# Up-projection in seven products: product 6 taken into the next pair, product 5 in a bank of its own, raw weights of odd pairs in other buffers

## The chip, the core and the metric

The kernel runs on one core of a Trainium2 chip. The core has five engines that work side by side and wait for each other by semaphores: TensorE (PE, matrix products into PSUM), VectorE (DVE), ScalarE (ACT), GpSimd (POOL) and SyncE (SP, which here issues the DMA transfers). Each engine takes its instructions in order. SBUF holds the tiles, PSUM has eight banks of 128 x 512 float32. The metric is the device time of one execution in microseconds (us); lower is better.

## What is computed

The reference is one decoder block on 1024 positions of width 1024: two token mixers (a gated linear attention and an indexed sparse attention), a gated MLP with a short convolution, and a gate with per-layer input, each followed by a layer norm. The change touches the up-projection of the MLP alone:

```python
h = causal_dwconv(x @ w_up[i], conv_w[i], conv_b[i])   # w_up: 1024 x 5632, conv over 3 positions
h_gate, h_val = jnp.split(h, 2, axis=-1)               # 2816 columns each
ffn = (jax.nn.silu(h_gate) * h_val) @ w_down[i]
x = layer_norm(DEEPNORM_ALPHA * x + ffn, ln2_g[i], ln2_b[i])
```

Everything is float32.

## The kernel before

**Precision.** A float32 product is made of three matmuls of a narrower float type: each operand is split into hi (ACT copies it into the narrower type, line 101) and lo (what is left, line 106, here on POOL), and `mm3` (L155 is the matmul) adds hi x hi, hi x lo and lo x hi in PSUM.

**Seven products.** The up-projection works on 22 pairs f of 128-column blocks, a gate block and its value block. A pair is a 2 x 2 block product (two column blocks, two halves of the 1024 positions, two halves of the inner dimension), done in Strassen's way (Winograd's form) with seven products in place of eight. Product j takes a weight part W[j] and an x part XS[j]; the XS are made once, at the end of the layer norm before. One product is 4 inner tiles of 3 matmuls, 12 matmuls of 512 columns, so a pair has 84.

**Weights of a pair** (`w_sets`). Two loads of 512 KB from w_up (line 991) go to two raw tiles wr, of which there are two in all. `left_operands` then alternates between splitting a raw quarter or a difference into hi and lo (put) and making the next difference in place on VectorE (line 164). The order of the parts is 0, 5, 1, 2, 3, 4, 6. There are seven sets of hi and lo tiles (wh and wl), so a part can be written when PE is done with the same part of the pair before.

**Products of a pair** (`up`). Three PSUM banks A, B, Dk (tag ch, eight banks in all). A takes product 0, and later 4 on top; B takes 1, then 3 on top, then 5 on top; Dk takes 2, then 6 on top. Between them the banks are read: s1 = copy of A (ACT, L1022), u2 = s1 + B, u3 = s1 + B after product 3, and four results go to the two halves of h (VectorE, `plus`, L1019; ACT, L1032). Since 3 is added to B, it waits for u2; since 5 is added to B, it waits for u3.

**Convolution** (`conv`). For either half of h: ACT makes the first tap with the bias (L1043), VectorE adds two shifted taps (L1045), the gate half goes through SiLU on ACT (L1048), POOL multiplies gate and value (L164, cv), and SP stores the result to d_act in DRAM (L1050). The last pair's convolution is put off into the next stage.

**Next stage.** The down-projection loads the stored activations into raw tiles ar (three of them, `rawp`), weights into dr, and splits both into units au and wu in the same manner; these lie where the x parts and weight parts were.

**What sets the order.** The kernel's text says what depends on what; a scheduler with its own time model then writes a fixed order for each engine, in which it may pull instructions ahead. So the order rows below and not the code alone tell what an engine does next.

Of the kernel before, what the change touches and what calls it, by code (L numbers as in the profile page):

```python
# [8 lines left out]
F32 = mybir.dt.float32  # L9
# [3 lines left out]
AF = mybir.ActivationFunctionType  # L13
ALU = mybir.AluOpType
# [3 lines left out]
P = 128  # L18
L = 1024
D = 1024  # L20
NT = L // P
KT = D // P
HALF = 512
# [5 lines left out]
NF = FF // P  # L29
# [11 lines left out]
def hybrid_block(ctx: ExitStack, tc: tile.TileContext, x, p, w_in, w_gate_up, b_gate, g_gla, w_gla,  # L41
                 g_ckv, w_uv, w_dsa, w_out, ln1_g, ln1_b, w_up, conv_w, conv_b, w_down, ln2_g, ln2_b,
                 w_ple, w_ple_gate, ln3_g, ln3_b, out, tap=None):
    nc = tc.nc
    V, S, G, T = nc.vector, nc.scalar, nc.gpsimd, nc.tensor
    tap = tap or (lambda name, ap: None)
    x, p, out = x[0], p[0, 0], out[0]
# [11 lines left out]
    wp = pool("wstream")  # L59
# [30 lines left out]
    def nm(s):  # L90
        uid[0] += 1
        return f"{s}_{uid[0]}"

    def bank(kind="mm", shape=(P, HALF)):
        return PS[kind].tile(list(shape), F32, name=nm(kind), tag=kind)
# [119 lines left out]
    def quad(a):  # L215
        return a.rearrange("p (a b) -> p a b", b=P)
# [16 lines left out]
    def run(steps):  # L233
        for f in steps:
            f()
# [64 lines left out]
    with ExitStack() as mix:  # L300
# [359 lines left out]
        with ExitStack() as c3:  # L660
# [138 lines left out]
            for h in range(DH):  # L799
                b = 4 * h - 2.0 * h / (DH - 1)  # L800
# [174 lines left out]
    with ExitStack() as c1:  # L975
        psum_banks(c1, "d", ch=8)
        fp = pool("ffwork", stack=c1)
        rawp = pool("raws", stack=segd, side="right")
        wk = pool("upwork", stack=segk, side="right")
        UE, UE0, US = 'GGGGGGG', 'VVGVVGV', 'VVVV'  # L980
        nset = [0]

        def blocks(f):

            return (NF + f, f) if f < NF - 1 else (f, NF + f)

        def w_sets(f):
            raw = []
            for c in blocks(f):
                raw.append(wp.tile([P, 1024], F32, name=nm("wr"), tag="wr", bufs=2))  # L990
                nc.sync.dma_start(raw[-1].rearrange("p (k c) -> p k c", k=KT), wup_v[:, :, c * P:(c + 1) * P])
            W = []
            for _ in range(7):
                n = nset[0] % 7
                nset[0] += 1
                pl, nb = (wq, 4) if n < 4 else (fp, 3)
                W.append([pl.tile([P, 512], F32R, name=nm(x), tag=x, bufs=nb) for x in ("wh", "wl")])
            run(left_operands(raw[1][:, :512], raw[1][:, 512:], raw[0][:, :512], raw[0][:, 512:],
                              lambda j, src: split(*W[j], src, "A", (UE if f else UE0)[j]), US))
            return [[quad(t) for t in w] for w in W]  # L1000

        def up(f):


            W = w_sets(f)
            h = wk.tile([P, 2, L], F32, name=nm("h"), tag="h")
            hv = [h[:, i].rearrange("p (a g q) -> p a g q", g=2, q=P) for i in range(2)]
            A, B, Dk = (bank("ch") for _ in range(3))

            def prod(ps, j, start):  # L1010
                for k in range(4):
                    mm3(ps, (W[j][0][:, k], W[j][1][:, k]), (XS[j][:, 0, k], XS[j][:, 1, k]), start and k == 0, k == 3,
                        not start)

            def tmp():
                return wk.tile([P, HALF], F32, name=nm("um"), tag="um", bufs=4)

            def plus(out, a, b):
                V.tensor_tensor(out=out, in0=quad(a), in1=quad(b), op=ALU.add)  # L1019
            prod(A, 0, True)  # L1020
            s1 = tmp()
            S.activation(s1, A, AF.Copy)  # L1022
            prod(B, 1, True)
            u2 = tmp()
            plus(quad(u2), s1, B)
            prod(Dk, 2, True)
            prod(B, 3, False)
            u3 = tmp()
            plus(quad(u3), s1, B)
            plus(hv[1][:, :, 1], u3, Dk)  # L1030
            prod(A, 4, False)
            S.activation(hv[0][:, :, 0], quad(A), AF.Copy)  # L1032
            prod(B, 5, False)
            plus(hv[1][:, :, 0], s1, B)
            prod(Dk, 6, False)
            plus(hv[0][:, :, 1], u2, Dk)

            def conv():
                out_ = {}
                for i in (1, 0):  # L1040
                    c = blocks(f)[1 - i]
                    o = out_[c // NF] = wk.tile([P, L], F32, name=nm("cv"), tag="cv", bufs=3)
                    S.activation(o, h[:, i], AF.Identity, bias=cbias[:, c:c + 1], scale=cw[:, 2, c:c + 1])  # L1043
                    for d in (1, 2):
                        V.scalar_tensor_tensor(o[:, d:], h[:, i, :L - d], cw[:, 2 - d, c:c + 1], o[:, d:], ALU.mult,  # L1045
                                               ALU.add)
                    if c < NF:
                        S.activation(o, o, AF.Silu)  # L1048
                sums(out_[0], out_[0], out_[1], ALU.mult, "G")
                nc.sync.dma_start(d_act[f // 6][:, f % 6], out_[0])  # L1050
            return conv

        for f in range(NF):
            last_conv = up(f)
            if f < NF - 1:
                last_conv()
    segx.close()
    sega.close()

# [244 lines left out]
```

## Time and profile before

| | us |
|---|---|
| median of 3 runs (lowest, highest) | 2181.69 (2181.13, 2181.78) |
| the profiled execution, its own time | 2181.69 |
| its span, first to last instruction | 2180.0 |
| up-projection, PE's stretch in the trace | 1306 to 1760 |

A timeline row has the start, the time of the merged run of equal instructions, the engine, the line of the kernel, the operation, output <- inputs by the program's names, sizes, the count, and in brackets the idle time of the engine before it with what ended it. PE's matmuls overlap: a row shows 0.39 us for one, but the next starts earlier, so the pace is read from start to start. VectorE's instructions overlap in the same way by less than 0.1 us. A wait is put down to the releaser that came last.

### The profile page before, as it was taken

To read this page: it belongs to the slowest core of one execution; us is meant where nothing else is said; L and a number is where in the kernel's file an instruction comes from. 1 tells how busy PE (TensorE), PEld (TensorE's weight loads), DVE (VectorE), ACT (ScalarE), POOL (GpSimd) and SP (SyncE) were. 2 spreads that over 40 slices of the span, in tenths; PEclk is the share of its full clock that TensorE was granted. 3 is DMA by queue.
4 is the path that set the end of the run, shared out by engine and by line. 5 is a ranking of instruction groups with operands and counts; after the bars stand their busy time and mean duration, and the time that the engine had idled before them with its cause. 6 is when DMAs were issued, how large, how long until landed. Compare 5 with 4: busy or idle time off the path is not lost.

```text
span 2180.0 us, 32423 instructions
## 1 busy us (share of the span) xinstructions
PE 2066.6 (95%) x12210; PEld 1813.0 (83%) x12210; DVE 1581.1 (73%) x2700; ACT 848.4 (39%) x1498; POOL 956.6 (44%) x808
## 2 busy tenths in 40 slices
PE   9999999999999999998999969999999968989897
PEld 8888899999988888887789967777777768989897
DVE  3489999999138888775243685666676689896965
ACT  4343212222127666665222343444334443332421
POOL 2433443543521212122332775555555655444743
PEclk9999999999999999999999979999999989999999
DMA  4222211211227767779666432232222224224222
GB/s 136 78 68 76 82 42 45 61 50 51 73 82 134 148 134 150 134 172 223 191 201 137 146 108 76 71 118 78 69 86 78 68 82 160 88 74 136 88 98 78
DMA packets 377565, 227.13 MB, mean 104 GB/s; under 512 B 189328, under 2 KB 351760, under 8 KB 377408
## 3 DMA queue, kind: packets, MB, share of 16 engines
q1 hardware_dynamic: 377408, 225.06, 38.2%
q8 instruction: 96, 1.57, 0.3%
q14 instruction: 61, 0.50, 0.1%
HBM read 146.37 MB, written 40.89 MB: 86 GB/s over the span
## 4 chain that ended last, share of the span: by engine, by line
PE 18%; DVE 16%; POOL 9%; DMA 6%; issue 4%; ACT 2%; SPq 0%; POOLq 0%; DVEq 0%; ACTq 0%
PE mm L155 12%; POOL wl L106 6%; DVE wr L164 5%; PE ch L155 5%; DMA wr<-in_w_up_dram 3%; DVE au L106 2%; ACT wh L101 2%; DVE wu L106 1%; DVE ar L164 1%; DVE um L164 1%; DMA wr<-d_ob 1%; DVE dr L164 1%; DVE res_all L1132 1%; DVE cv L1045 1%; POOL lnmv L212 1%
## 5 line engine op out<-in xcount | busy, mean ns | idle before, releaser
L106 POOL TENSOR_TENSOR wl<-wr,wh 128x512 fp32r<-128x512 f32 x381 | 524.9, 1393 | 439.9 <-ACT wh L101 425.2
L155 PE MATMUL ch<-xs,wh 128*128 128x512 f32 x1232 | 385.3, 395 | 33.2 <-DVE um L1019 26.2
L155 PE MATMUL mm<-Ah,wh 128*128 128x512 f32 x832 | 331.6, 399 | 2.0 <-ACT wh L101 1.1
L155 PE MATMUL mm<-Al,wh 128*128 128x512 f32 x832 | 330.4, 397 | 0.8 <-DVE Al L106 0.5
L155 PE MATMUL mm<-Ah,wl 128*128 128x512 f32 x832 | 329.3, 396 | 0.0
L155 PEld LDWEIGHTS ch<-xs,wh 128*128 128x128 f32 x1232 | 231.5, 190 | 91.2 <-DVE um L1019 35.1
L101 ACT ACTIVATE wh<-wr 128x512 fp32r<-128x512 f32 (+1 forms) x278 | 166.9, 625 | 347.1 <-DVE wr L164 144.5
L103 POOL TENSOR_SCALAR wh<-wr 128x512 fp32r<-128x512 f32 x112 | 77.0, 690 | 382.2 <-PE mm L155 211.9
L155 PE MATMUL ch<-xs,wl 128*128 128x512 f32 x616 | 240.8, 392 | 0.8 <-POOL wl L106 0.6
L155 PE MATMUL ch<-wu,au 128*128 128x256 f32 x1512 | 195.1, 291 | 32.3 <-DVE um L164 9.9
L155 PE MATMUL mm<-wl,Ah 128*128 128x256 f32 x768 | 217.6, 285 | 4.5 <-POOL wl L106 4.3
L155 PEld LDWEIGHTS ch<-wu,au 128*128 128x128 f32 x1512 | 189.5, 198 | 38.0 <-DVE um L164 12.1
L155 PE MATMUL mm<-wh,Al 128*128 128x256 f32 x768 | 216.3, 284 | 0.0
L155 PE MATMUL mm<-wh,Ah 128*128 128x256 f32 x768 | 213.8, 284 | 0.0
L155 PEld LDWEIGHTS mm<-Ah,wl 128*128 128x128 f32 x832 | 156.2, 188 | 32.9
L155 PEld LDWEIGHTS mm<-Ah,wh 128*128 128x128 f32 x832 | 156.3, 188 | 32.8 <-ACT wh L101 1.6
L155 PEld LDWEIGHTS mm<-Al,wh 128*128 128x128 f32 x832 | 156.4, 188 | 31.3 <-DVE Al L106 0.9
L651 DVE MATCH_REPLACE8 score<-m,score 128x896 f32<-128x896 f32 (+3 forms) x192 | 166.4, 869 | 0.0
L650 DVE MAX8 m<-score 128x8 f32<-128x896 f32 (+3 forms) x192 | 163.5, 875 | 2.3 <-POOL score L457 2.1
L164 DVE TENSOR_TENSOR wr<-wr,wr 128x512 f32<-128x512 f32 x66 | 88.8, 1346 | 93.9 <-POOL wl L106 93.7
L155 PEld LDWEIGHTS mm<-wl,Ah 128*128 128x128 f32 x768 | 145.7, 190 | 6.2 <-POOL wl L106 5.5
L155 PE MATMUL mm<-wh,au 128*128 128x256 f32 x768 | 144.3, 284 | 2.6 <-ACT wh L101 1.4
(259 smaller groups left out, 4221.0 us busy)
## 6 DMA issues: line engine op xcount, KB each, us to landing
wr<-in_w_in_dram SPq DMA_DIRECT2D x60, 512.0 KB, 3.9
wr<-in_w_up_dram SPq DMA_DIRECT2D x44, 512.0 KB, 3.9
d_act<-cv SPq DMA_DIRECT2D x22, 512.0 KB, 2.6
dr<-in_w_down_dram SPq DMA_DIRECT2D x12, 768.0 KB, 6.4
ar<-d_act SPq DMA_DIRECT2D x12, 768.0 KB, 5.2
d_tg<-tg SPq DMA_DIRECT2D x32, 256.0 KB, 2.0
wr<-in_w_out_dram SPq DMA_DIRECT2D x16, 512.0 KB, 3.6
wr<-in_w_ple_gate_dram SPq DMA_DIRECT2D x16, 512.0 KB, 4.2
```

The costliest lines, as they stand in the source:

```text
L101: S.activation(dst, src, AF.Copy, scale=scale)
L103: (V if eng == "V" else G).tensor_scalar(dst, src, scale, 0.0, ALU.mult, ALU.add)
L106: done["GV"[eng != "G"]] = (G if eng == "G" else V).tensor_tensor(out=dst, in0=src, in1=hi.bitcast(F32), op=ALU.subtract)
L155: T.matmul(ps, lhsT=l, rhs=r, start=start, stop=stop, skip_group_check=more)
L164: (G if eng == "G" else V).tensor_tensor(out=out, in0=a, in1=b, op=op)
L212: G.tensor_scalar(dst, src, scale, eps, ALU.mult, ALU.add)
L650: V.max(m8, score[t])
L651: V.match_replace(score[t], m8, score[t], TAKEN)
L1045: V.scalar_tensor_tensor(o[:, d:], h[:, i, :L - d], cw[:, 2 - d, c:c + 1], o[:, d:], ALU.mult, ALU.add)
L1132: V.scalar_tensor_tensor(rv, rv, ALPHA, src, ALU.mult, ALU.add)
```

## The change

Raw weights of odd pairs are loaded into the ar tiles instead of wr. A pair now uses four banks: product 5 has its own (C). The pair's steps are functions that the loop puts in a row: products 0 and 1 of a pair, then product 6 of the pair before, product 5, the convolution of the pair before's block 0, products 2, 3, 4, and the convolution of the pair's block 1, which is complete after product 3. The um tiles go; the results are summed in place in h, which is two tiles per pair with two buffers each.

```diff
@@ -987,7 +987,11 @@
         def w_sets(f):
             raw = []
             for c in blocks(f):
-                raw.append(wp.tile([P, 1024], F32, name=nm("wr"), tag="wr", bufs=2))
+                if f % 2:
+                    raw.append(rawp.tile([P, 6, 256], F32, name=nm("ar"), tag="ar", bufs=3)
+                               .rearrange("p a b -> p (a b)")[:, :1024])
+                else:
+                    raw.append(wp.tile([P, 1024], F32, name=nm("wr"), tag="wr", bufs=2))
                 nc.sync.dma_start(raw[-1].rearrange("p (k c) -> p k c", k=KT), wup_v[:, :, c * P:(c + 1) * P])
             W = []
             for _ in range(7):
@@ -1002,58 +1006,81 @@
         def up(f):
 
 
+
+
             W = w_sets(f)
-            h = wk.tile([P, 2, L], F32, name=nm("h"), tag="h")
-            hv = [h[:, i].rearrange("p (a g q) -> p a g q", g=2, q=P) for i in range(2)]
-            A, B, Dk = (bank("ch") for _ in range(3))
+            st, out_ = {}, {}
 
             def prod(ps, j, start):
                 for k in range(4):
                     mm3(ps, (W[j][0][:, k], W[j][1][:, k]), (XS[j][:, 0, k], XS[j][:, 1, k]), start and k == 0, k == 3,
                         not start)
 
-            def tmp():
-                return wk.tile([P, HALF], F32, name=nm("um"), tag="um", bufs=4)
-
             def plus(out, a, b):
-                V.tensor_tensor(out=out, in0=quad(a), in1=quad(b), op=ALU.add)
-            prod(A, 0, True)
-            s1 = tmp()
-            S.activation(s1, A, AF.Copy)
-            prod(B, 1, True)
-            u2 = tmp()
-            plus(quad(u2), s1, B)
-            prod(Dk, 2, True)
-            prod(B, 3, False)
-            u3 = tmp()
-            plus(quad(u3), s1, B)
-            plus(hv[1][:, :, 1], u3, Dk)
-            prod(A, 4, False)
-            S.activation(hv[0][:, :, 0], quad(A), AF.Copy)
-            prod(B, 5, False)
-            plus(hv[1][:, :, 0], s1, B)
-            prod(Dk, 6, False)
-            plus(hv[0][:, :, 1], u2, Dk)
-
-            def conv():
-                out_ = {}
-                for i in (1, 0):
-                    c = blocks(f)[1 - i]
-                    o = out_[c // NF] = wk.tile([P, L], F32, name=nm("cv"), tag="cv", bufs=3)
-                    S.activation(o, h[:, i], AF.Identity, bias=cbias[:, c:c + 1], scale=cw[:, 2, c:c + 1])
-                    for d in (1, 2):
-                        V.scalar_tensor_tensor(o[:, d:], h[:, i, :L - d], cw[:, 2 - d, c:c + 1], o[:, d:], ALU.mult,
-                                               ALU.add)
-                    if c < NF:
-                        S.activation(o, o, AF.Silu)
+                V.tensor_tensor(out=out, in0=a, in1=quad(b), op=ALU.add)
+
+            def p0():
+                st["A"] = bank("ch")
+                prod(st["A"], 0, True)
+                st["h"] = [wk.tile([P, L], F32, name=nm("h"), tag=f"h{i}", bufs=2) for i in range(2)]
+                st["hv"] = [h.rearrange("p (a g q) -> p g a q", g=2, q=P) for h in st["h"]]
+                S.activation(st["hv"][1][:, 0], quad(st["A"]), AF.Copy)
+
+            def p1():
+                st["B"] = bank("ch")
+                prod(st["B"], 1, True)
+                plus(st["hv"][0][:, 1], st["hv"][1][:, 0], st["B"])
+
+            def p5():
+                st["C"] = bank("ch")
+                prod(st["C"], 5, True)
+
+            def p2():
+                st["D"] = bank("ch")
+                prod(st["D"], 2, True)
+
+            def p3():
+                prod(st["B"], 3, False)
+                s1, u3 = st["hv"][1][:, 0], st["hv"][1][:, 1]
+                plus(u3, s1, st["B"])
+                plus(s1, u3, st["C"])
+                plus(u3, u3, st["D"])
+
+            def p4():
+                prod(st["A"], 4, False)
+                S.activation(st["hv"][0][:, 0], quad(st["A"]), AF.Copy)
+
+            def p6():
+                prod(st["D"], 6, False)
+                o = st["hv"][0][:, 1]
+                plus(o, o, st["D"])
+
+            def conv(i):
+                c = blocks(f)[1 - i]
+                h = st["h"][i]
+                o = out_[c // NF] = wk.tile([P, L], F32, name=nm("cv"), tag="cv", bufs=3)
+                S.activation(o, h, AF.Identity, bias=cbias[:, c:c + 1], scale=cw[:, 2, c:c + 1])
+                for d in (1, 2):
+                    V.scalar_tensor_tensor(o[:, d:], h[:, :L - d], cw[:, 2 - d, c:c + 1], o[:, d:], ALU.mult, ALU.add)
+                if c < NF:
+                    S.activation(o, o, AF.Silu)
+
+            def conv1():
+                conv(1)
+
+            def conv0():
+                conv(0)
                 sums(out_[0], out_[0], out_[1], ALU.mult, "G")
                 nc.sync.dma_start(d_act[f // 6][:, f % 6], out_[0])
-            return conv
-
+            return p0, p1, p5, p2, p3, p4, conv1, p6, conv0
+
+        late = []
         for f in range(NF):
-            last_conv = up(f)
-            if f < NF - 1:
-                last_conv()
+            p0, p1, p5, p2, p3, p4, conv1, *rest = up(f)
+            run([p0, p1, *late[:1], p5, *late[1:], p2, p3, p4, conv1])
+            late = rest
+        late[0]()
+        last_conv = late[1]
     segx.close()
     sega.close()
 
```

On PE, the place is where product 0 of the next pair ends, in the middle of the stage (ch_14675 is bank B of a pair, xs_11727 the x part of product 0, xs_12438 that of product 5). Before:

```order
L155 MATMUL ch_14819<-xs_11727,wl_14787 128x512
L155 MATMUL ch_14819<-xs_11727,wh_14786 128x512 x2
L155 MATMUL ch_14819<-xs_11727,wl_14787 128x512
L155 MATMUL ch_14675<-xs_12438,wh_14651 128x512 x2
L155 MATMUL ch_14675<-xs_12438,wl_14652 128x512
```

After (ch_14802 is bank B of this pair, ch_14829 its bank C, ch_14705 bank D of the pair before; xs_11728 belongs to product 1, xs_12439 to product 6):

```order
L155 MATMUL ch_14786<-xs_11727,wl_14755 128x512
L155 MATMUL ch_14802<-xs_11728,wh_14756 128x512 x2
L155 MATMUL ch_14829<-xs_12438,wh_14764 128x512 x2
L155 MATMUL ch_14829<-xs_12438,wl_14765 128x512
L155 MATMUL ch_14829<-xs_12438,wh_14764 128x512
L155 MATMUL ch_14705<-xs_12439,wh_14622 128x512
L155 MATMUL ch_14802<-xs_11728,wl_14757 128x512
```

Before, product 0 of the next pair stood between products 3 and 5 of a pair; now product 0 is followed by the start of products 1 and 5 of its own pair and product 6 of the pair before, and bank B takes only products 1 and 3.

On VectorE, one pair's round in the middle of the stage (ch_14675 is bank B, ch_14676 bank Dk; wr_14784 and wr_14782 are the raw weights of the pair that follows). Before:

```order
L164 TENSOR_TENSOR wr_14784<-wr_14784,wr_14782 128x512
L164 TENSOR_TENSOR wr_14782<-wr_14782 128x512
L1019 TENSOR_TENSOR um_14729<-um_14689,ch_14675 128x512
L164 TENSOR_TENSOR wr_14782<-wr_14782,wr_14784 128x512
L1019 TENSOR_TENSOR h_14673<-um_14729,ch_14676 128x4x128
L1019 TENSOR_TENSOR h_14673<-um_14689,ch_14675 128x4x128
L164 TENSOR_TENSOR wr_14784<-wr_14784,wr_14782 128x512
L1045 SCALAR_TENSOR_TENSOR cv_14771<-h_14673,cw,cv_14771 128x1023
```

After (wr_14752 and wr_14750 are the raw weights of the pair that follows; h_14511 and cv_14698 belong to the pair before; ch_14658, ch_14685, ch_14705 are banks B, C, D):

```order
L164 TENSOR_TENSOR wr_14752<-wr_14752,wr_14750 128x512
L164 TENSOR_TENSOR wr_14750<-wr_14750 128x512
L1020 TENSOR_TENSOR h_14655<-h_14656,ch_14658 128x4x128
L1020 TENSOR_TENSOR h_14511<-h_14511,ch_14561 128x4x128
L1064 SCALAR_TENSOR_TENSOR cv_14698<-h_14511,cw,cv_14698 128x1023
L1064 SCALAR_TENSOR_TENSOR cv_14698<-h_14511,cw,cv_14698 128x1022
L164 TENSOR_TENSOR wr_14750<-wr_14750,wr_14752 128x512
L1020 TENSOR_TENSOR h_14656<-h_14656,ch_14658 128x4x128
L1020 TENSOR_TENSOR h_14656<-h_14656,ch_14685 128x4x128
L1020 TENSOR_TENSOR h_14656<-h_14656,ch_14705 128x4x128
L1064 SCALAR_TENSOR_TENSOR cv_14746<-h_14656,cw,cv_14746 128x1023
L1064 SCALAR_TENSOR_TENSOR cv_14746<-h_14656,cw,cv_14746 128x1022
```

The two first differences of the next pair's weights stood ahead of u3; now they stand ahead of the add of product 1, and the three adds behind product 3 stand in one piece with the block's taps behind them.

On POOL, the same round after (wl_14623 is lo part 6 of a pair, the other wl are the parts of the pair that follows in the order 0, 5, 1, 2, 3, 4, cv_14698 the product of gate and value of the pair before):

```order
L106 TENSOR_TENSOR wl_14755<-wr_14752,wh_14754 128x512
L106 TENSOR_TENSOR wl_14623<-ar_14608,wh_14622 128x512
L106 TENSOR_TENSOR wl_14765<-wr_14750,wh_14764 128x512
L164 TENSOR_TENSOR cv_14698<-cv_14698,cv_14602 128x1024
L106 TENSOR_TENSOR wl_14757<-wr_14750,wh_14756 128x512
L106 TENSOR_TENSOR wl_14759<-wr_14750,wh_14758 128x512
L106 TENSOR_TENSOR wl_14761<-wr_14752,wh_14760 128x512
L106 TENSOR_TENSOR wl_14763<-wr_14752,wh_14762 128x512
```

Before, all seven parts of a pair stood together and the product of gate and value behind the first part of the next pair; now part 6 comes behind that first part, and the product two places later.

## Rows read from the trace of the kernel before

**Rows 1.** The page: busy us, share of the span and count by engine.

```profile
PE 2066.6 (95%) x12210; PEld 1813.0 (83%) x12210; DVE 1581.1 (73%) x2700; ACT 848.4 (39%) x1498; POOL 956.6 (44%) x808
```

**Rows 2.** Windows: stretch, length, busy us (count) by engine, clock, DMA.

```profile
1306.00:1760.00 454.00, 426.54 (x1837) 344.56 (x1838) 303.75 (x284) 185.76 (x262) 255.35 (x170) 0.99 0.25 79
1760.00:1796.00 36.00, 20.40 (x111) 18.79 (x111) 35.77 (x32) 15.33 (x27) 26.39 (x16) 0.76 0.31 102
```

**Rows 3.** Timeline of PE: pace, one hole, the regular hole's first and last.

```profile
1365.47 0.73 PE L155 MATMUL ch<-xs,wh 128*128 128x512 f32 x2 [1.35 <-DVE um L1019]
...
1499.98 0.39 PE L155 MATMUL ch<-xs,wl 128*128 128x512 f32 x1
...
1507.46 0.39 PE L155 MATMUL ch<-xs,wl 128*128 128x512 f32 x1
1509.11 0.73 PE L155 MATMUL ch<-xs,wh 128*128 128x512 f32 x2 [1.25 <-DVE um L1019]
...
1737.00 0.73 PE L155 MATMUL ch<-xs,wh 128*128 128x512 f32 x2 [1.32 <-DVE um L1019]
```

**Rows 4.** Timeline of PE at the start of the stage.

```profile
1306.46 1.65 PE L155 MATMUL ch<-xs,wh 128*128 128x512 f32 x3 [3.83 <-ACT xs L101]
...
1309.62 1.06 PE L155 MATMUL ch<-xs,wh 128*128 128x512 f32 x2
```

**Rows 5.** Waits from 1360 to 1740 us: total, times, longest.

```profile
DVE wr L164 <- POOL wl L106: 84.3, 37, 4.4
ACT wh L101 <- DMA wr<-in_w_up_dram: 58.9, 19, 3.6
...
PE ch L155 <- DVE um L1019: 24.6, 18, 1.8
```

**Rows 6.** Timelines of VectorE and of POOL, 1502 to 1520 us.

```profile
1503.89 2.87 DVE L164 TENSOR_TENSOR wr<-wr,wr 128x512 f32<-128x512 f32 x1 [1.76 <-POOL wl L106]
1506.79 1.67 DVE L164 TENSOR_TENSOR wr<-wr 128x512 f32<-128x512 f32 x1
1508.38 0.67 DVE L1019 TENSOR_TENSOR um<-um,ch 128x512 f32<-128x512 f32 x1
...
1515.48 0.69 DVE L164 TENSOR_TENSOR wr<-wr,wr 128x512 f32<-128x512 f32 x1 [2.63 <-POOL wl L106]
1516.09 1.28 DVE L1045 SCALAR_TENSOR_TENSOR cv<-h,cw,cv 128x1023 f32<-128x1023 f32 x1
...
1517.88 1.71 DVE L1045 SCALAR_TENSOR_TENSOR cv<-h,cw,cv 128x1022 f32<-128x1022 f32 x1
...
1503.81 2.40 POOL L164 TENSOR_TENSOR cv<-cv,cv 128x1024 f32<-128x1024 f32 x1
1506.17 1.75 POOL L106 TENSOR_TENSOR wl<-wr,wh 128x512 fp32r<-128x512 f32 x1
1510.40 2.55 POOL L106 TENSOR_TENSOR wl<-wr,wh 128x512 fp32r<-128x512 f32 x2 [2.49 <-ACT wh L101]
...
1516.98 1.54 POOL L106 TENSOR_TENSOR wl<-wr,wh 128x512 fp32r<-128x512 f32 x1 [1.53 <-ACT wh L101]
```

**Rows 7.** Timeline of ACT, from the same stretch.

```profile
1497.49 1.25 ACT L1043 ACTIVATE cv<-h,cbias,cw 128x1024 f32<-128x1024 f32 x1 [1.18 <-DVE h L1019]
1501.80 0.63 ACT L101 ACTIVATE wh<-wr 128x512 fp32r<-128x512 f32 x1 [3.06 <-DMA wr<-in_w_up_dram]
...
1522.90 1.05 ACT L1048 ACTIVATE cv<-cv 128x1024 f32<-128x1024 f32 x1
```

**Rows 8.** SP's issues in the timeline; the page's loads (KB, us to landing).

```profile
1516.20 2.71 SPq L991 DMA_DIRECT2D wr<-in_w_up_dram  x2
...
wr<-in_w_up_dram SPq DMA_DIRECT2D x44, 512.0 KB, 3.9
```

**Rows 9.** Timeline of VectorE at the end of the stage and behind it.

```profile
1757.44 0.69 DVE L1019 TENSOR_TENSOR h<-um,ch 128x512 f32<-128x512 f32 x1 [2.38 <-PE ch L155]
...
1782.83 3.21 DVE L1045 SCALAR_TENSOR_TENSOR cv<-h,cw,cv 128x1023 f32<-128x1023 f32 x2
```

## The prediction

> **What bounds the kernel now.** I read the page first: TensorE (PE) is busy for 95% of the span [rows 1], so a gain must show as PE time, and since matmuls overlap, the busy share hides what PE loses inside a stage. Next come the windows: the up-projection with its 22 pairs runs from 1306 to 1760 us, 454.0 us with 1837 matmuls (of 1848), at a granted clock of 0.99 of the upper level, 2.4 GHz [rows 2].
>
> The timeline of PE gives the pace and the hole. From 1499.98 to 1507.46 us there are 33 matmuls, 0.2267 us each [rows 3]. A pair has 84 (seven products of 12), so PE needs 19.04 us for it. The hole is at 1509.11, where the next matmul should have begun at 1507.46 + 0.23 = 1507.69: 1.42 us lost, released by VectorE's um of line 1019 [rows 3]. The same hole stands at 1365.47 and 1737.00, 18 pairs apart [rows 3], so a pair takes 371.53 / 18 = 20.64 us and loses 1.60.
>
> For the whole stage: 1837 x 0.2267 = 416.4 us. The first 13 matmuls run at the lower clock: seven of them take from 1306.46 to 1309.62 us [rows 4], 0.45 each, 0.22 more than later, 2.9 in all. 454.0 - 416.4 - 2.9 = **34.7 us** in which PE has nothing to run. 18 x 1.60 = 28.8 of it are the regular holes, the rest lies in the first three pairs and the last.
>
> The waits between 1360 and 1740 us say why [rows 5]: PE waits for um 18 times. VectorE waits for POOL's lo parts 37 times, and ACT 19 times for a weight load. In rows: ACT has waited 3.06 us for a load when it starts at 1501.80 [rows 7], POOL's lo part follows, VectorE takes two differences of the next pair's raw weights (1503.89 and 1506.79), and only behind them the add u3 at 1508.38 [rows 6]. u3 reads bank B after product 3, and product 5 accumulates onto the same bank. That is the hole. The load itself is late because there are two raw buffers: it goes out when the pair before has let go of them, at 1516.20 for the next pair [rows 8].
>
> **The change part by part.**
>
> *Raw weights.* The loads keep number and size (44 of 512 KB, 3.9 us to landing [rows 8]). An odd pair's raw weights now go to two of three ar buffers, so a pair's load waits for the pair two before it. Those buffers are let go when part 6 is split, which waits for PE's third product in the row (3 x 2.72 = 8.2, and 2 for hi and lo): some 11 us into a pair. The first need is ACT's split of part 0 behind the first product of the next pair, 22 us from the same start. What hides the landing is these 11 us; without that cover the 1.60 us a pair stay. On SP's queue the d_act stores now stand behind these loads, but a store has most of a pair's time before its cv buffer (three of them) is wanted again, so I cost that at 0. The other bound is one issue, 2.71 / 2 = 1.4 us [rows 8], in every pair, 30 us, as if all of it stood in PE's way.
>
> *Banks and order on PE.* Product 5 gets a bank of its own and product 6 moves behind product 1 of the next pair; the order shows 5 and 6 between the pieces of 1. The count of matmuls is the same. Bank B must now be read (add 1) only before product 3, and 6, 5 and 2 stand in between: 3 x 2.72 = 8.2 us of cover. Eight banks hold two pairs of four.
>
> *Adds and copies.* VectorE has five adds a pair in the code as before, each with one operand in PSUM (0.67 us, and the next instruction starts about 0.6 behind such a one [rows 6]); ACT copies two banks as before. One add works in place, which no row shows. Bounds: 0.60 as its neighbours, 1.28 as an instruction of two SBUF operands [rows 6]; I take 0.60, the nearer form, because its second operand is still PSUM. At 1.28 it would cost 0.68 a pair on the loop below.
>
> *What is late next.* With hole and load gone, PE (19.04) races a loop of VectorE, ACT and POOL, whose orders are fixed. First the price of their overlap. VectorE's difference of two SBUF operands began at 1503.89 beside POOL's product (1503.81 to 1506.21) and ended at 1506.76, 0.55 behind it; POOL's lo part then ended 1.16 after that; VectorE's next 0.54 after that one; a conv tap (1517.88) ended at 1519.59, 1.07 behind POOL's 1518.52 [rows 6]. So they take turns, at 0.55 (difference), 1.07 (tap) and 1.15 (lo part) once they have waited; alone these are 0.69, 1.28 and 1.27. Now a pair by the new orders, t = 0 at the end of POOL's first lo part for the coming pair. VectorE: a12 difference 0.55, the two first differences, add 1 and add 6 at 0.60 each, 2.95. ACT's conv pass 1.25 [rows 7] with 0.1 each for the hand-over: 4.35. First tap 1.25 more: 5.65. lo part 5 behind it: 6.8. Second tap: 7.9. SiLU 1.05 [rows 7]: 9.0. POOL's gate x value product 2.40: 11.5. lo part 1: 12.65. Then in turns tap, lo 2, tap, lo 3 (1.07 + 1.15 twice): 17.1. lo 4 and the next first part, 1.25 each: **19.6 us a pair**.
>
> That is 0.56 above PE's 19.04. It does not hit at once: walked in the same way from a start without backlog, PE's product 6 (third in the row, 9.1 us after the pair began) opens the round: add 6 to 9.95, conv pass 11.3, taps with lo part 5 between them 14.8, SiLU 15.95, product 18.4, lo part 1 at 19.6 us; PE wants it at 19.04 + 2.72 (product 0) + 7 x 0.2267 (the seven matmuls in front of it) = 23.35. 3.75 us of slack at about 0.5 a pair last 7 to 8 pairs; with the first two, ten pairs run at PE's pace and twelve pay 0.56: 6.7 us.
>
> At this place stands a rule of the Trainium skill (SBUF — State Buffer, Who interferes with whom): VectorE with two SBUF inputs and a GpSimd instruction that reads SBUF share one read port, and the second is blocked until the first ends. The order of the ends above agrees with it, the 0.55 behind the release against 0.69 alone do not quite: part of the work goes on while it waits. Taken strictly it gives the slower rival below. Another of its rules (TensorE: Matmul & The Clock Gate, Wait — 56ns, not 53.3ns?) puts 512-column matmuls at 215.7 ns apart when warm; the rows here have 226.7, and the measured one stands. By that page of the Trainium skill, PE would want 18.1 us a pair and the loop would bind from the first pair, at 22 x 0.56 = 12 us instead of 6.7.
>
> *Both ends of the stage.* At the start PE waits 3.83 us for x's operands [rows 4]. In the new order VectorE makes x's last difference some three instructions earlier. Bounds 0 and 3.8 gained; I take 0, nearest to the row, because the last operand still comes through the same three engines. At the end the down-projection is prepared by a VectorE that is busy for 35.77 of 36 us [rows 2]. Two of its four taps there (3.21 for two [rows 9]) now run before PE ends, but they and the three adds of product 3 push the preparation back by about as much (VectorE stood idle for 2.38 us before 1757.44 [rows 9], and will wait for ACT's 1.25 in its place). I take 0, bounds 3.2 either way. The first d_act loads of the down-projection find their ar buffers taken until the last pair; the two that matter first can go some 10 us before PE ends, and at half again a w_up load's size they take some 6 us by its 3.9 [rows 8], so 0 too, 6 if they came late.
>
> Sum: 34.7 - 6.7 = 28.0 us off. The profiled execution took 2181.69 us (span 2180.0 and 1.69 around it), which is also the median of the runs. 2181.69 - 28.0 = 2153.7, **2154 us**.
>
> **The rivals.**
> - *PE's pace throughout.* The turns cost less than walked, the loop stays under 19.04 and all 34.7 us go: 2147. For it: add and product do not collide in all pairs. Against: the walk counts no other delay.
> - *The loop is longer.* Two or three more collisions bring it to about 20.2. Backlog grows by 1.16 a pair, the slack lasts three pairs, about 18 pay 1.16: 21 us, 14 left, 2168.
> - *The change doesn't do what it says:* the seven sets of parts are still one per product, so a part waits until PE has used its forerunner; if that keeps the splits late as today, PE loses its 1.60 in another place: 2182. Against it: the part of product 1 has 3.75 us of slack, and every other part more.
> - *Slower: strict turns.* Where the second of two colliding instructions takes its whole time alone after the wait, the same walk has 0.69, 1.28 and 1.27 in place of 0.55, 1.07 and 1.15, and gives 21.2 us. Backlog grows by 2.2 a pair, so after two pairs VectorE's add 1, queued behind two differences that wait for POOL, holds product 3 back. 2 x 19.04 + 20 x 21.2 = 462 us, plus 2.9 at the lower clock, for 454: 2181.69 + 11 = 2193. The point from which it decides is a loop of 20.7 us. This is the Trainium skill's rule (SBUF — State Buffer, Who interferes with whom) to the letter. The rows have the shorter ends in four of four collisions, against it.
>
> **How the numbers follow.** Forecast 0.62 (its own range 2148 to 2161: backlog paid by no or by all pairs, and one bound of an end), PE's pace 0.14, longer loop 0.14, no effect 0.04, slower 0.06. The range 2146 to 2168 holds the forecast, PE's pace and the shorter half of the longer loops, and leaves out under 2 in 10. A measurement of this kernel tells about 0.2%, 4.4 us, from no change. Faster: 0.62 + 0.14 + 0.14 + a little of the fourth, 0.91; same 0.03; slower 0.06.
>
> **What would show it.** Right: no PE wait on an add in front of product 5; no ACT wait on a load of w_up behind the third pair; PE dense, 0.2267 from matmul to matmul, in the first pairs after the start; later a short PE wait per pair (about half a us) on a lo part or on add 1; stage of 454 - 28 = 426 us. Wrong: a pair period at 19.04 to the end (then the turns are cheaper), or above 20; PE waits on ACT's hi parts (then the sets of parts bind); a transition to the down-projection that differs by over 3 us.

## The result, and the profile after

The changed kernel took 2157.73 us (median of 4 runs, 2155.79 to 2158.16), the kernel before 2181.74 beside it (2181.13 to 2185.19): ratio 0.9884, 95% interval 0.9873 to 0.9896, 24.0 us less. Forecast were 2154 us and 28.0 less. The profiled execution has a span of 2156.2 us. Its page begins (busy us, share of the span, count by engine):

```profile
PE 2067.9 (96%) x12210; PEld 1815.2 (84%) x12210; DVE 1585.9 (74%) x2700; ACT 841.9 (39%) x1498; POOL 996.8 (46%) x808
```

Against [rows 1] every count stands as it was and PE's busy time nearly so (1.3 us more); POOL is busy longer by 40 us, VectorE by 5. A turn that an instruction waits out counts as its busy time: four lo parts beside two taps take 6.99 us in the round below, 1.75 each, and 1.28 alone.

The waits from 1360 to 1720 us answer to [rows 5] (who waited for whom: us in total, times, longest):

```profile
...
ACT wh L101 <- DVE ar L164: 59.5, 9, 6.7
ACT cv L1066 <- DVE cv L1064: 56.5, 18, 3.4
DVE cv L1064 <- ACT cv L1062: 50.3, 37, 1.5
POOL cv L164 <- issue: 40.5, 17, 2.6
ACT cv L1062 <- DVE h L1020: 34.4, 18, 1.9
DVE ar L164 <- POOL wl L106: 21.9, 9, 2.4
...
PE ch L155 <- POOL wl L106: 6.5, 16, 0.7
PEld ch L155 <- DVE h L1020: 4.1, 16, 0.3
```

ACT's 58.9 us of waiting for w_up's loads are gone, and so are PE's 18 waits for an add. In their place VectorE, ACT and POOL wait for one another, and PE waits 16 times for POOL's lo part. Its weight loads (PEld) also wait 16 times for a short moment for VectorE's add 1, in front of product 3; PE is 0.1 us late there. Where a wait is put down to "issue", the profile saw no releaser: in the round below POOL's product starts 0.13 us after SiLU ends. The timelines of PE and of its weight loads (start, us, instruction, idle before it and what ended that) show where, and answer to [rows 3, 4]:

```profile
1302.39 2.69 PE L155 MATMUL ch<-xs,wh 128*128 128x512 f32 x5 [4.13 <-ACT wh L101]
...
1399.22 0.19 PEld L155 LDWEIGHTS ch<-xs,wl 128*128 128x128 f32 x1 [0.55 <-POOL wl L106]
...
1419.11 0.50 PE L155 MATMUL ch<-xs,wl 128*128 128x512 f32 x1 [0.42 <-POOL wl L106]
...
1717.56 0.50 PE L155 MATMUL ch<-xs,wl 128*128 128x512 f32 x1 [0.38 <-POOL wl L106]
...
1734.92 0.39 PE L155 MATMUL ch<-xs,wl 128*128 128x512 f32 x1
1735.73 0.50 PE L155 MATMUL ch<-wu,au 128*128 128x256 f32 x2 [0.42 <-ACT au L101]
```

For five pairs, until 1399.22, PE waits for nothing; then once a pair, with a period of (1717.56 - 1419.11) / 15 = 19.90 us, 0.86 over its own 19.04. From product 1 of the first pair to the start of the last matmul this stage takes 1734.92 - 1302.39 = 432.53 us. The same two marks in the kernel before are 1306.46 and 1759.74, 453.28 us. So the stage gained 20.75 us; it began 4.07 us earlier, and what lies behind it took 1.02 more (421.28 for 420.26): 23.8 us, the difference of the spans.

One round of the three engines in the middle of the changed kernel's stage, from their timelines, in order of start:

```profile
1603.90 1.29 POOL L106 TENSOR_TENSOR wl<-wr,wh 128x512 fp32r<-128x512 f32 x1
1603.98 1.76 DVE L164 TENSOR_TENSOR ar<-ar,ar 128x512 f32<-128x512 f32 x1 [2.43 <-POOL wl L106]
...
1606.99 1.28 DVE L1020 TENSOR_TENSOR h<-h,ch 128x512 f32<-128x512 f32 x2
1608.38 1.24 ACT L1062 ACTIVATE cv<-h,cbias,cw 128x1024 f32<-128x1024 f32 x1 [1.91 <-DVE h L1020]
...
1609.66 3.52 DVE L1064 SCALAR_TENSOR_TENSOR cv<-h,cw,cv 128x1023 f32<-128x1023 f32 x2 [1.39 <-ACT cv L1062]
...
1613.27 1.06 ACT L1066 ACTIVATE cv<-cv 128x1024 f32<-128x1024 f32 x1 [3.12 <-DVE cv L1064]
...
1614.46 2.41 POOL L164 TENSOR_TENSOR cv<-cv,cv 128x1024 f32<-128x1024 f32 x1 [2.37 <-issue]
...
1616.83 6.99 POOL L106 TENSOR_TENSOR wl<-wr,wh 128x512 fp32r<-128x512 f32 x4
...
1617.13 4.30 DVE L1064 SCALAR_TENSOR_TENSOR cv<-h,cw,cv 128x1023 f32<-128x1023 f32 x2 [1.31 <-ACT cv L1062]
...
1623.79 1.28 POOL L106 TENSOR_TENSOR wl<-ar,wh 128x512 fp32r<-128x512 f32 x1
```

Read it as one chain: lo part, difference, adds, conv pass, taps, SiLU (L1066), product of gate and value, four lo parts with two taps among them (6.99 us), and the next first lo part at its end, 1625.07; the first one ended at 1605.19. That is 19.88 us, and PE's work does not set the round: POOL's products stand 19.9 us apart from the first one in this stage (1335.82 us) on, before PE waits for anything. PE needs the first of the four lo parts, and gets it once in 19.9 us.

### The profile page after: what moved, and what is told of

The parts are those of the page before. It is cut to its first block, busy times and chain, and to the rows that moved or that the text cites. A ratio compares the mean times of both kernels' runs of the same rounds, so it can differ in the third digit from the quotient of the medians.

```text
span 2156.2 us, 32472 instructions
## 1 busy us (share of the span) xinstructions
PE 2067.9 (96%) x12210; PEld 1815.2 (84%) x12210; DVE 1585.9 (74%) x2700; ACT 841.9 (39%) x1498; POOL 996.8 (46%) x808
## 4 chain that ended last, share of the span: by engine, by line
PE 22%; DVE 12%; POOL 8%; issue 7%; DMA 2%; ACT 2%; SPq 0%; POOLq 0%; DVEq 0%; ACTq 0%
PE mm L155 12%; PE ch L155 10%; POOL wl L106 5%; DVE au L106 2%; DVE cv L1064 1%; DVE wu L106 1%; DVE um L164 1%; DVE h L1020 1%; DVE dr L164 1%; DMA wr<-d_ob 1%; DVE ar L164 1%; ACT cv L1062 1%; DVE res_all L164 1%; POOL lnmv L212 1%; DMA dr<-in_w_down_dram 1%
## 5 line engine op out<-in xcount | busy, mean ns | idle before, releaser
L106 POOL TENSOR_TENSOR wl<-wr,wh 128x512 fp32r<-128x512 f32 x304 | 439.9, 1460 | 287.3 <-ACT wh L101 279.7
L1064 DVE SCALAR_TENSOR_TENSOR cv<-h,cw,cv 128x1023 f32<-128x1023 f32 x88 | 167.6, 1905 | 59.9 <-ACT cv L1062 58.4
L101 ACT ACTIVATE wh<-wr 128x512 fp32r<-128x512 f32 (+1 forms) x201 | 120.6, 622 | 186.7 <-PE mm L155 77.0
L106 POOL TENSOR_TENSOR wl<-ar,wh 128x512 fp32r<-128x512 f32 x77 | 127.7, 1677 | 44.9 <-ACT wh L101 44.9
```

Source lines behind the costliest of these rows:

```text
L101: S.activation(dst, src, AF.Copy, scale=scale)
L106: done["GV"[eng != "G"]] = (G if eng == "G" else V).tensor_tensor(out=dst, in0=src, in1=hi.bitcast(F32), op=ALU.subtract)
L1064: V.scalar_tensor_tensor(o[:, d:], h[:, :L - d], cw[:, 2 - d, c:c + 1], o[:, d:], ALU.mult, ALU.add)
```

## Experiments

Each kernel ran beside the kernel before (there 2181.65 to 2182.11 us), and the ratio is to that one. "Stage" is measured as above, from the start of product 1 to the start of the last matmul, in each kernel's trace.

| kernel | us | ratio, 95% interval | stage |
|---|---|---|---|
| before | 2181.74 | 1 | 453.3 |
| changed | 2157.73 | 0.9884, 0.9873 to 0.9896 | 432.5 |
| e1 raw buffers alone | 2180.74 | 0.9993, 0.9984 to 1.0002 | 450.1 |
| e2 bank and order alone | 2187.65 | 1.0023, 1.0014 to 1.0031 | 460.5 |
| e3 changed, no product | 2142.75 | 0.9818, 0.9806 to 0.9831 | 418.6 |
| e4 changed, product on VectorE | 2148.65 | 0.9842, 0.9829 to 0.9854 | 418.9 |
| e5 before, product on VectorE | 2160.79 | 0.9901, 0.9883 to 0.9919 | 435.1 |
| e6 e1, product on VectorE | 2163.13 | 0.9913, 0.9900 to 0.9927 | 437.6 |
| e7 changed, product 6 not late | 2150.03 | 0.9852, 0.9838 to 0.9865 | 423.7 |
| e8 changed, lo part 1 on VectorE | 2165.64 | 0.9925, 0.9912 to 0.9937 | 439.8 |
| e9 changed, product 6 behind 0 | 2150.54 | 0.9851, 0.9838 to 0.9865 | 422.5 |
| e10 e2, product on VectorE | 2160.15 | 0.9898, 0.9885 to 0.9912 | 431.9 |
| e11 e7, product on VectorE | 2146.08 | 0.9833, 0.9818 to 0.9847 | 418.0 |

The order on the engines is laid out anew for every kernel, so an edit moves more than its own lines. Only e9 is nearly clean: POOL's order is that of the changed kernel word for word.

**e1: the first half alone.** The change's edit of `w_sets`, with `up` as before.

```diff
+                if f % 2:
+                    raw.append(rawp.tile([P, 6, 256], F32, name=nm("ar"), tag="ar", bufs=3) ...
```

> The first half of the change alone: odd pairs' raw weights in ar buffers, banks and order of products as in the kernel before. Theory A (two causes, one hole): the hole of 1.60 us a pair is VectorE's add u3, held back behind two differences of the next pair's raw weights that in turn wait for late loads; with early loads the differences are done in time, product 0 of the next pair still stands between products 3 and 5 and covers the add, and only the loop of VectorE, ACT and POOL at 19.9 us a pair is left: 2155 to 2163 us, no ACT wait on a load after the third pair, PE waits on lo parts or short ones on adds. Rival B (the bank is the cause): product 5 still accumulates onto bank B, so the add stays in PE's way and most of the 1.60 us stays: 2172 to 2182 us.

Rival B's time, but not by its mechanism. PE does not wait for the add any more, it waits for ACT's hi parts (timelines of all four engines):

```profile
1521.62 1.06 ACT L1052 ACTIVATE cv<-cv 128x1024 f32<-128x1024 f32 x1 [3.40 <-DVE cv L1049]
...
1522.81 2.39 POOL L164 TENSOR_TENSOR cv<-cv,cv 128x1024 f32<-128x1024 f32 x1 [2.37 <-PE ch L155]
...
1525.16 1.26 POOL L106 TENSOR_TENSOR wl<-ar,wh 128x512 fp32r<-128x512 f32 x1
...
1526.46 0.69 DVE L164 TENSOR_TENSOR ar<-ar,ar 128x512 f32<-128x512 f32 x1 [4.93 <-POOL wl L106]
...
1527.19 1.67 ACT L101 ACTIVATE wh<-ar 128x512 fp32r<-128x512 f32 x3 [3.50 <-DVE ar L164]
...
1527.87 1.21 PE L155 MATMUL ch<-xs,wh 128*128 128x512 f32 x4 [2.75 <-ACT wh L101]
```

The next pair's raw weights are there, but its first lo part stands behind POOL's product, the difference behind the lo part, the hi parts behind the difference, and PE behind those. From 1320 to 1720 us PE waits seven times in this way, 19.4 us in all. With the load's wait gone this chain holds PE up instead, and the stage gained only 3.2 us.

**e2: the second half alone.** The changed kernel with the `wr` line for every pair.

> The second half alone: product 5 in its own bank, product 6 in the next pair, all raw weights in the two wr buffers. Theory A: the load for the next pair goes out when part 6 is split, some 11 us into a pair, lands 6.6 us later (3.9 and 2.7), and ACT wants it some 22 us from the start, so the raw buffers hide it: within 4 us of the whole change, 2154 to 2162 us. Rival B: without the third and fourth raw buffer ACT waits 2 to 3 us a pair for a load as before, and since the loop of VectorE, ACT and POOL is already 0.86 us over PE's 19.04, each us of that wait shows: 2180 us or more.

Rival B. ACT waits for loads again, and the stage is 7.2 us longer than before (waits from 1360 to 1720 us):

```profile
ACT wh L101 <- DMA wr<-in_w_up_dram: 59.7, 27, 6.9
...
PE ch L155 <- DVE h L1016: 13.3, 6, 3.2
```

PE itself waits most for an add of VectorE. One such place in the timelines shows how the load gets there: ACT's hi part waits for the load, POOL's lo part for the hi part, VectorE's differences for the lo part, one of them is stretched to 2.28 us beside POOL's product, and the add comes behind them:

```profile
1567.22 0.63 ACT L101 ACTIVATE wh<-wr 128x512 fp32r<-128x512 f32 x1 [0.94 <-DMA wr<-in_w_up_dram]
...
1570.15 2.89 POOL L164 TENSOR_TENSOR cv<-cv,cv 128x1024 f32<-128x1024 f32 x1
...
1571.31 2.28 DVE L164 TENSOR_TENSOR wr<-wr 128x512 f32<-128x512 f32 x1
...
1575.92 0.73 PE L155 MATMUL ch<-xs,wh 128*128 128x512 f32 x2 [3.24 <-DVE h L1016]
```

So my 11 us of cover for a load hold only with the four raw buffers of the change; with two, the load goes out too late. Neither half alone is worth anything (e1 is level with the kernel before, e2 takes 5.5 us longer), both together are worth 20.75 us of the stage.

**e3 and e4: what the rest of the loss is.** In e3 the product of gate and value is left out, the gate alone is stored; in e4 VectorE makes it:

```diff
-                sums(out_[0], out_[0], out_[1], ALU.mult, "G")
+                sums(out_[0], out_[0], out_[1], ALU.mult, "V")
```

> The changed kernel with the product of gate and value left out (the gate alone is stored). Theory A (the rest of the loss is the fixed-order loop of 19.9 us a pair, in which POOL's product stands between SiLU and the lo parts): without it the lo parts follow ACT's hi parts at once, the loop falls to about 18, below PE's 19.04, PE runs dense to the end of the stage: 13 us less than the changed kernel, 2143 to 2147 us, no regular PE wait on a lo part. Rival B (PE waits because a set of parts comes free late, or the turns of VectorE and POOL bind by their sum, not by the chain): the period stays at 19.5 or more: 2153 us or more.

> The changed kernel with the product of gate and value on VectorE in place of POOL. Theory A: the lo parts no longer wait behind SiLU; VectorE takes 1.3 to 1.4 us more a pair and has some 15 of 19.04 to do, its own round through ACT (taps, SiLU, product, three adds, conv pass, taps, differences, two adds, conv pass) walks to about 15.3: PE's pace throughout, 2143 to 2148 us. Rival B: VectorE, now waiting for SiLU in front of the three adds of product 3 and taking turns with POOL more often, becomes the loop: 2158 us or more.

Theory A's mechanism in both; the times lie 0.3 us below its range (e3) and 0.7 above it (e4). In neither, from 1330 to 1720 us, do PE or its weight loads wait for anything that the trace shows; the stage of 418.61 and 418.89 us, 418.75 in the mean, is PE's own pace. One round of e4 (timelines):

```profile
1603.59 1.06 ACT L1066 ACTIVATE cv<-cv 128x1024 f32<-128x1024 f32 x1 [2.54 <-DVE cv L1064]
...
1604.69 1.23 DVE L164 TENSOR_TENSOR cv<-cv,cv 128x1024 f32<-128x1024 f32 x1 [0.59 <-ACT cv L1066]
1605.25 4.33 POOL L106 TENSOR_TENSOR wl<-wr,wh 128x512 fp32r<-128x512 f32 x3 [2.83 <-ACT wh L101]
...
1606.03 2.13 DVE L1020 TENSOR_TENSOR h<-h,ch 128x512 f32<-128x512 f32 x3
```

The product takes 1.23 us on VectorE (2.41 on POOL), and the lo parts follow ACT's hi parts while VectorE still multiplies. The changed kernel had 432.53 - 418.75 = 13.8 us left to lose, and both ways of taking the product out of POOL's round give all of it.

**e5, e6 and e10: the product's part in the old hole.** The same edit on the kernel before, on e1 and on e2.

> The kernel before with one edit: the product of gate and value on VectorE in place of POOL; neither half of the change. Theory A (the hole of 1.60 us a pair is made by POOL's product as much as by the late load: it begins 0.08 us before VectorE's first difference, which then takes 2.87 in place of 0.69, and the lo part behind it stretches the next from 0.68 to 1.67, 3.2 us in front of the add u3): without it u3 comes some 2 us earlier less 1.3 for the product itself, the hole shrinks to 0.3 to 0.9: 2160 to 2172 us. Rival B (the load sets u3's time): ACT still waits about 3 us for it, hole as before, and the product is one more thing in front of u3: 2178 us or more.

> Raw weights of odd pairs in ar buffers and the product of gate and value on VectorE; banks and order of products as in the kernel before. Theory A (the raw buffers alone brought nothing because POOL's product stood in front of part 0's lo part, on which a difference, ACT's hi parts and then PE waited, 2.75 us each time): with the product off POOL that chain is gone and PE runs at its pace, 2144 to 2152 us, so the bank of its own and the late product 6 are not needed then. Rival B (product 5 on bank B still needs the add u3 in time): a hole of 0.3 to 1 us a pair stays, 2155 to 2170 us.

> Product 5 in its own bank and product 6 in the next pair, all raw weights in the two wr buffers, and the product of gate and value on VectorE. Theory A (the load binds here: with two raw buffers ACT waits 2 to 7 us for loads, whatever POOL does): a stage of 435 to 455 us, 2160 to 2180 us, ACT waits on loads in every pair. Rival B (POOL's product was the cause here too): PE's pace, stage 419 to 425 us, 2144 to 2151 us.

e5: theory A. The one edit gives 18.1 us of the stage, nearly as much as the whole change, though ACT still waits for loads (58.9 us in the 380 us of [rows 5]; here from 1340 to 1720 us):

```profile
ACT wh L101 <- DMA wr<-in_w_up_dram: 65.7, 19, 5.5
```

The late load was a part of the hole's chain, but the hole goes without touching it. PE still waits here, no longer for the add but for ACT's hi parts (9 times, 7.0 us from 1330 to 1720 us). What went are the long first differences beside POOL's product: 2.87 in [rows 6], and so in 18 rounds of the kernel before; in e5 in none:

```profile
1479.83 0.69 DVE L164 TENSOR_TENSOR wr<-wr,wr 128x512 f32<-128x512 f32 x1 [1.83 <-POOL wl L106]
```

e6: rival B's time, and again by another mechanism: PE waits 19 times for ACT's hi parts, 10.0 us in all, never for the add. With the raw buffers but without the bank, the product's place makes no more than 12.5 us. e10: theory A in kind (ACT waits 77.6 us for loads from 1340 to 1720 us), its stage of 431.9 us a little below the range. PE waits there ten times for an add of VectorE, 6.0 us in all. In one round (1534 to 1541 us) SiLU stands on ACT behind a hi part that waited 3.22 us for its load, VectorE's product behind SiLU, and the add behind the product. PE reaches its own pace only where the raw buffers, the bank of product 5 and a POOL without the product come together (e3, e4, and e11 below).

**e8: a lo part less on POOL.** `UE` is 'GVGGGGG'.

> The changed kernel with the lo part of product 1 split on VectorE in place of POOL, the product of gate and value still on POOL. Theory A (the loop is a chain, one lo part of 1.25 to 1.75 us behind the product less makes it shorter than PE's 19.04): the period falls to 18 to 19, PE's pace nearly throughout, 2143 to 2150 us. Rival B (the lo part, now behind two taps on VectorE, takes 0.7 to 1.2 there in front of the three adds, and only moves the chain): the period stays at 19.5 to 20, 2154 to 2160 us.

Rival B, and worse than it: PE's weight loads wait for this lo part at 1605.29 and 1625.54, 20.25 us a round. The lo part takes its turn behind POOL's product (timelines):

```profile
1602.30 2.38 POOL L164 TENSOR_TENSOR cv<-cv,cv 128x1024 f32<-128x1024 f32 x1 [2.64 <-issue]
...
1602.72 2.52 DVE L106 TENSOR_TENSOR wl<-ar,wh 128x512 fp32r<-128x512 f32 x1 [1.38 <-ACT wh L101]
...
1605.16 2.12 DVE L1020 TENSOR_TENSOR h<-h,ch 128x512 f32<-128x512 f32 x3
```

It lasts 2.52 us, ends 0.56 behind the product, and the three adds, the conv pass and the taps all stand behind it. The move took 27 us of busy time off POOL (298.9 to 272.1 in the stage) and put 32 on VectorE, the busier of the two (312.6 to 344.6), and the lo part stayed in the chain.

**e7, e9 and e11: the order of two adds.** In e7 product 6 runs in its own pair; in e9 it stays late but goes one place ahead:

```diff
-            run([p0, p1, *late[:1], p5, *late[1:], p2, p3, p4, conv1])
+            run([p0, *late[:1], p1, p5, *late[1:], p2, p3, p4, conv1])
```

> The changed kernel, but product 6 and what follows it in its own pair again; the bank of product 5 and the raw buffers as changed. Theory A: VectorE, ACT and POOL have the same round in nearly the same order (only the adds of products 6 and 1 change places), so the loop of 19.9 us a pair binds as before, and since product 6 is done earlier the slack is larger: 2150 to 2160 us. Rival B (the late product is what covers the adds and lets the round start): without it PE waits on adds or hi parts in every pair, 2165 us or more.

> The changed kernel with product 6 of the pair before put behind product 0 in place of behind the start of product 1. On VectorE this swaps two adds (that of product 6 now ahead of that of product 1); POOL's order is untouched. Theory A (the round's chain runs difference, add 1, add 6, conv pass, taps, and add 1 is in it only because it stands first): the conv pass starts one add sooner, the round falls from 19.88 to 19.28 us, stage 8 to 12 us shorter than in the changed kernel: 2146 to 2152 us, rounds of POOL's product 19.3 us apart. Rival B (what shortened the round when product 6 went back to its own pair was PE's earlier product, not the order of the adds): 19.9 as in the changed kernel, 2156 to 2159 us.

e7 gave theory A's time for a wrong reason: I put it down to slack, but the round itself is shorter: POOL's products stand 19.3 us apart there. e9 tells why: POOL's products stand 19.30 and 19.28 us apart, 0.60 less than in the changed kernel, as forecast, and VectorE waits less for the conv pass:

```profile
1591.49 2.41 POOL L164 TENSOR_TENSOR cv<-cv,cv 128x1024 f32<-128x1024 f32 x1 [2.64 <-issue]
...
1610.79 2.41 POOL L164 TENSOR_TENSOR cv<-cv,cv 128x1024 f32<-128x1024 f32 x1 [2.37 <-issue]
...
1630.07 2.40 POOL L164 TENSOR_TENSOR cv<-cv,cv 128x1024 f32<-128x1024 f32 x1 [2.37 <-issue]
...
1603.91 1.28 DVE L1020 TENSOR_TENSOR h<-h,ch 128x512 f32<-128x512 f32 x2
1605.98 3.52 DVE L1064 SCALAR_TENSOR_TENSOR cv<-h,cw,cv 128x1023 f32<-128x1023 f32 x2 [0.80 <-ACT cv L1062]
```

The conv pass needs add 6 alone. With add 1 in front of it (1.39 us of idle in the changed kernel's round above, 0.80 here) a whole add stood in the chain for nothing. PE's earlier product 6 is not the reason: in the changed kernel's round VectorE does not stand idle in front of either add. The stage is 10.1 us shorter for a swap of two names. Of the change's three parts the late product 6, as it was placed, is thus the one that cost time: with it back in its own pair (e7) the stage is 8.9 us shorter.

> Bank and raw buffers as changed, product 6 in its own pair, the product of gate and value on VectorE: both edits that beat the changed kernel, together. Theory A (with either the stage is within 5 us of PE's own pace, 418.9 with the product on VectorE, so nothing is left to add): stage 418 to 420 us, 2143 to 2149 us, the same as with the product on VectorE alone. Rival B (VectorE's product, waiting for SiLU in front of the three adds, hurts once product 6 is not late): stage 422 us or more, 2150 us or more.

Theory A: 418.0 us of stage, with product 6 not late, 2146.08 us, the lowest median of those that compute everything. Whether it beats e4 (2148.65, 2145.45 to 2150.26) the runs do not tell (2142.48 to 2147.62), and by the stage there is nothing left to gain.

## Why the prediction came out as it did

**Hole and load gone: right.** No PE wait on an add in front of product 5 is left, and no ACT wait on a load of w_up. PE's own pace was right too: 34.7 us of loss forecast, 453.28 - 418.75 = 34.5 measured with e3 and e4. The Trainium skill has 215.7 ns from start to start for back-to-back matmuls of 512 columns once warm (TensorE: Matmul & The Clock Gate, Wait — 56ns, not 53.3ns?). The same two stages do not reach it: between the two marks 1835 matmuls begin, each with a weight load of its own, and (418.75 - 2.9 at the lower clock) / 1835 = 0.2266 us. Whether they would reach it without the weight loads no run here shows.

**The cause of the hole: half right.** I told it as the late load's chain. e1 takes the load's wait away and leaves most of the loss, in another place; e5 leaves the wait and takes 18.1 us of the loss away. The rows had it: POOL's product begins 0.08 us before VectorE's difference and holds it back [rows 6]. I used these rows for the price of turns and not for the cause.

**The fixed-order loop: the step that was mis-sized.** Its mechanism is shown by e3, e4 and e9, and each link came within 0.3 us of the walk. Forecast was **19.6 us** a pair, measured 19.88 to 19.90. Walk against the round above, both from the end of the first lo part: adds done 2.95 and 3.08; taps 7.9 and 7.99; SiLU 9.0 and 9.14; product 11.5 and 11.68; the four lo parts 18.35 and 18.63; next lo part 19.6 and 19.88. The 0.28 is no single collision: 0.13 up to the adds, 0.10 at the four lo parts, the rest in between.

**From there the rest of the miss follows.** The loss a pair is 0.84 to 0.86, not 0.56, so a slack of 3.75 us would have lasted 3.75 / 0.86 = 4.4 pairs behind the first two, not seven or eight. PE waited sooner still, after five pairs (1399.22), where its next two matmuls came 0.29 and 0.11 us late. Counted back over three rounds, the slack in the third pair was about 3 x 0.85 - 0.4 = 2.1 us (an estimate), not 3.75: this term was mis-sized too. Seventeen pairs pay, 0.4 us in the first and about 0.85 in each of the other sixteen, 14.0 us, for 13.8 measured, against 12 x 0.56 = 6.7 forecast. Being 1.4% wrong on the loop makes the larger part of this, since only its excess over PE counts, and the excess counts twice: as price and as the speed at which the slack goes. That the forecast still held to 4 us is in part luck, as the next paragraph says.

**Both ends at 0: right within their bounds.** Behind the stage 421.28 us for 420.26, 1.0 more; over the eleven experiments it was 416.4 to 424.7. The stage began 4.07 us earlier, but product 0 to product 1 took 8.7 us in both (from 1297.73 and 1293.71), so the shift is from further up, in code that the change does not touch. Over all thirteen profiled executions product 1 began between 1302.39 and 1307.00. One part is seen: from 990 to 1110 us PE waited 4.2 us for a transfer of pt before, 1.5 after. So the forecast's 28.0 against 24.0 us measured flatters the walk: in the stage it was 28.0 against 20.75. How much of the other 3 us comes from the change and how much from the spread of executions stays open.

**Strict turns: refuted.** The Trainium skill has the second of two instructions on the shared port blocked until the first ends (SBUF — State Buffer, Who interferes with whom). The order of the ends agrees in every overlap of a tap or a difference with a lo part in the changed kernel's stage. The price is not: the difference ended 1605.74 - 1605.19 = 0.55 us behind the lo part, not the 0.69 that it takes alone, and the round stayed below the 20.7 us from which that rival decides. The 21.2 us that I gave that rival do not come out of its own prices: one difference, three taps and four lo parts at their full time add 0.14 + 3 x 0.21 + 4 x 0.12 = 1.25 us to 19.6, which makes 20.85, still slower than the kernel before. Its warning holds all the same: e8 shows what a collision in the wrong place costs.

## What to carry to other kernels

When PE stands close to a round of other engines, walk that round link by link and forecast a range for it, since a few tenths of a microsecond in it become the whole rest of the gain. Ask of each instruction in such a round whether the next link needs it or only stands behind it: the swap of two adds, and a product moved to another engine, were worth 10 and 14 us of stage. And test the parts of a change together before dropping one: here each half alone gave nothing, because a wait that the other half takes away kept PE back. Then take single parts out of the whole: the late product 6 turned out to cost more than it gave.

## What the runs showed of the hardware

A product of 128 x 1024 elements with two operands in SBUF took 2.41 us on POOL and 1.23 on VectorE (e4), and on POOL it also stretched VectorE's instruction beside it from 0.69 to 2.87 [rows 6] or, with a lo part in its place, from 0.68 to 2.52 us (e8). So its place cost the other engine nearly as much as its own length.
